# RWKV mixer of a hybrid decoder step: plain fp32 projections with r projected per pair, and chunk inverses doubled without VectorE transposes

## The chip, the cores and the metric

The program runs on one core of a Trainium2 chip. The metric is the device time of one launch in microseconds. TensorE (PE in the rows) multiplies, VectorE (DVE), ScalarE (ACT) and GpSimd (POOL) work on tiles of 128 partitions, SyncE (SP) issues most transfers. Every engine takes its own instructions in order; semaphores hold one until another engine is done.

## The reference, cut to what matters

One step of a two-layer trunk for 304 tokens: 16 meta and 256 prompt tokens of one sequence, and 8 samples of 4 tokens. The change is in the odd layer's mixer (RWKV-7); the even layer and the two PEER retrieval stages stay as they are.

```python
def rwkv7_mixer(x, s0, shift, ...):
    x_prev = jnp.concatenate([shift[:, None, :].astype(x.dtype), x[:, :-1]], axis=1)
    xx = x_prev - x
    xr, xw, xk, xv, xa, xg = (x + xx * mu[i] for i in range(6))
    r = xr @ w_r
    w = -jax.nn.softplus(-(w0 + jnp.tanh(xw @ w1) @ w2).astype(F32)) - 0.5
    k = xk @ w_k
    v = xv @ w_v
    a = jax.nn.sigmoid(a0 + (xa @ a1) @ a2)
    g = jax.nn.sigmoid(xg @ g1) @ g2
    ...
    y, s_new = wkv7_scan(rh, decay, kh, vh, -kk, kk * ah, s0)
    ...
    out = (y * g).astype(x.dtype) @ w_o
```

The scan is S = S diag(w) + (S a) b^T + v k^T, y = S r, for 16 heads of 64 channels. The kernel computes it in chunks of 64 tokens; in a chunk the (S a) terms are the solution of a triangular system, whose inverse the kernel builds.

## The kernel before, in words

Activations lie with 128 of 1024 channels on the partitions and the 304 tokens along the row; a weight block is 8 tiles of 128x128, 512 KB (`raw`). A product of full precision is made in one of two ways. Split: `wtile` (L243) and `split` (L169) make a rounded fp32r part and a residual of weights (`wh`, `wl`) and of activations (`mixh`, `mixl`), with ACT for the rounding and VectorE or GpSimd for the residual, and `mm3` (L174) makes three products. Plain: one fp32 product, which the trace shows as two passes.

`mixer1` (L1201) follows the layer normalization of the retrieval stage before it. Its prologue computes the six token-shift mixes (`blend`, L1348): k and v stay plain (`xk`, `xv`), the others are split. All eight r projections, the low-rank projections of w and a (one block) and that of g are made here in split form, then k, v and the preparation of pair 0.

The main part goes over eight pairs of heads with six generators per pair: `kv` (L1381, plain projections of k and v), `prep` (L1285, decays, normalized keys, `AR`, `BK`, `uv`), `attend` (L1470, products inside chunks), `inverse` (L1516), `chain` (L1591, the serial pass over five chunks) and `tail` (normalization and gate). Each step of each generator has a due number, pair + n0 + n1 * step (`self.mp`, L199), and the steps are issued in the order of these; the tile framework then places instructions in each engine's order. 144 small bf16 products into `ps_pj` (`warm`, L278) keep TensorE at work between them.

`inverse` works on three groups of the five chunks (2, 2 and 1 blocks of 128x128, two heads in each). It doubles the size of the inverted diagonal blocks in steps, on a matrix and its transpose (`ZV`), with a masked transposed block `t` (`tx`) as weights. The transposed block comes from a VectorE transpose of 32x32 squares out of PSUM (L1559), masked by a second VectorE instruction (L1560); the last steps use smaller transposes (L1564, L1572, L1574). At the end one correction step (L1584, L1588) refines the result. PSUM has eight banks: three of them (`iv`) serve the inverse, the attention products and part of the preparation in turn, two `ch`, and one each `mm`, `pu` and `pj`.

Of the kernel before, what the change touches and what calls it, by code (L numbers as in the profile page):

```python
# [8 lines left out]
F32 = mybir.dt.float32  # L9
# [11 lines left out]
P = 128  # L21
# [18 lines left out]
def _consts():  # L40
# [39 lines left out]
    for j in range(2):  # L80
# [11 lines left out]
        [ma[0].reshape(P, P), ma[1].reshape(P, P), lv[:, 0].T, lv[:, 1:5].reshape(P, 4 * P)], axis=1).astype(np.float32)  # L92
# [89 lines left out]
class Prog:  # L182
    def __init__(self, tc, a, es):
# [15 lines left out]
        self.mp = dict(q0=-3.6, q1=.12, p0=-3.0, p1=.14, a0=-2.2, a1=.14, i0=-1.45, i1=.2, c0=0, c1=.24, t0=1.5, t1=.15,  # L199
# [55 lines left out]
    def fetch(self, srcs):  # L255

        nc, tl = self.nc, lambda tag, dt: self.t(self.strm, [P, KB, P], dt, tag, 2)
        raws = [tl("raw", F32) for _ in srcs]
        for r, src in zip(raws, srcs):
            nc.sync.dma_start(r, src)  # L260

        def pre():
            self.turn.update(raw=-1, wh=1, wl=1)
            for j, r in enumerate(raws):
                h, l = tl("wh", F32R), tl("wl", F32R)
                split(nc, r, h, l, nc.gpsimd if j == 0 else None)
                self.ready.append((h, l))
        return pre
# [467 lines left out]
    def peer(self, xh, xl, l):  # L736
# [8 lines left out]
        with ExitStack() as es:  # L745
# [439 lines left out]
            pre = None if last else self.fetch([a["w_r"][j] for j in range(2)])  # L1185
# [15 lines left out]
    def mixer1(self, x, norm):  # L1201
        nc, a = self.nc, self.a
        with ExitStack() as es:
# [11 lines left out]
            masks = tl([P, 7, P], "masks", 1, BF16)  # L1215
            amask, lm0t, lmask = [masks[:, j, :] for j in range(2)], masks[:, 2, :], [masks[:, 2 + j, :] for j in range(5)]
# [18 lines left out]
            xkv = tl([P, KB, T], "xk"), tl([P, KB, T], "xv")  # L1235
# [49 lines left out]
            def prep(p):  # L1285
                AR, BK, uv = ARs[p % 6], BKs[p % 6], uvs[p % 6]
# [59 lines left out]
            mix, slot = {}, {0: 0, 1: 1, 4: 2, 5: 1}  # L1346

            def blend(i, k):  # L1348

                whole = 1 < i < 4  # L1350
                m = xkv[i - 2][:, k, :] if whole else ta([P, T], "sq", 3)
                nc.vector.scalar_tensor_tensor(m, xx[:, k, :], vec(7 + i, k), x[:, k, :], op0=ALU.mult, op1=ALU.add)  # L1352
                if whole:
                    return
                if k == 0:
                    mix[i] = tuple(ta([P, KB, T], f"{n}{slot[i]}", 1, F32R) for n in ("mixh", "mixl"))
                mh, ml = mix[i]
                split(nc, m, mh[:, k, :], ml[:, k, :], None if k % 4 == 1 else nc.gpsimd)

            srcs = [a["w_r"][p] for p in range(KB)] + [a["w_l1"][1]]  # L1360
            srcs.insert(5, a["w_l1"][0])
            tiles = []

            def weights():

                while len(tiles) < 3 and srcs:
                    tiles.append(self.wtile(srcs.pop(0), nc.gpsimd if len(srcs) % 3 == 0 else None))
                return tiles.pop(0)

            turn = [0]  # L1370

            def proj(w, i, c0=0, c1=P):
                turn[0] += 1
                ps = self.psum(("mm", "iv", "iv", "iv")[turn[0] % 4])
                wh, wl = w
                mh, ml = mix[i]
                mm3(nc, ps[:c1 - c0, :T], lambda k: wh[:, k, c0:c1], lambda k: wl[:, k, c0:c1],
                    lambda k: mh[:, k, :], lambda k: ml[:, k, :])
                return ps

            def kv(p):  # L1381

                for j, n in enumerate(("w_k", "w_v")):
                    w = self.stream("raw", F32)
                    nc.sync.dma_start(w, a[n][p])
# [5 lines left out]
                    nc.scalar.activation(Vts[p % 2][:, :T] if j else Kt[:, p, :], ps, AF.Copy)  # L1391
                    yield

            steps = [(i, k) for i in (1, 4, 2, 3, 5) for k in range(KB)]

            def ahead(n):
                for _ in range(n):
                    if steps:
                        blend(*steps.pop(0))


            ws, pr = [self.wtile(srcs.pop(0)) for _ in range(2)], [self.psum("iv") for _ in range(2)]
# [10 lines left out]
            def r(p, n):  # L1413
                ps = pr[p] if p < 2 else proj(weights(), 0)
                nc.scalar.activation(R[:, p, :], ps[:, :T], AF.Copy)
                ahead(n)

            r(0, 1)
            r(1, 1)
            for p in (2, 3, 4):  # L1420
                r(p, 5)
            w = weights()
            for i, c in ((1, 0), (4, 64)):
                ps = proj(w, i, c, c + 64)
                nc.scalar.activation(hwa[c:c + 64], ps[:64, :T], AF.Copy if c else AF.Tanh)
                ahead(4)
            gens = {}
            gens["q", 0], gens["p", 0] = kv(0), prep(0)
            for _ in range(5):
                next(gens["q", 0], None)  # L1430
                ahead(3)
            for p in (5, 6, 7):
                next(gens["p", 0], None)
                r(p, 4)
            ps = proj(weights(), 5)
            nc.scalar.activation(hg, ps[:, :T], AF.Sigmoid)
            for _ in gens["p", 0]:
                pass
            nc.vector.tensor_copy(psh.unsqueeze(2), x[:, :, TP - 1:TP])
# [11 lines left out]
            TX = 5  # L1451
            GROUPS = ((0, 2), (2, 2), (4, 1))

            for j in (2, 3, 4, 5, 1):
# [7 lines left out]
            X5s = [[tb([P, 2, P], f"x5{i}{j}") for j in range(2)] for i in range(2)]  # L1462
            for x5, X in X5s:
                nc.gpsimd.tensor_copy(x5, self.ident[:, None, :].to_broadcast([P, 2, P]))
                nc.gpsimd.memset(X, 0.0)
# [4 lines left out]
            def attend(p):  # L1470

                AR, BK, NT = ARs[p % 6], BKs[p % 6], NTs[p % 3]
# [41 lines left out]
                st[p] = AR, uvs[p % 6], AT, BT, NT, Ts, SA, SR  # L1514

            def inverse(p):  # L1516


                NT = NTs[p % 3]
                Zo = BKs[p % 6].rearrange("p c a t -> p c (a t)")  # L1520
                st[p] += (Zo,)
                wh, wl = self.t(self.strm, [P, KB, P], F32R, "wh", 2), self.t(self.strm, [P, KB, P], F32R, "wl", 2)
                flat = lambda ap: ap.rearrange("p c t -> p (c t)")
                gs = []
                for c0, n in GROUPS:
# [7 lines left out]
                    gs.append([c0, n, NR, ZV, t])  # L1533
                yield
                for j in range(6):
                    for g in gs:
                        c0, n, NR, ZV, t = g
# [3 lines left out]
                        bc = lambda ap: ap[:, None, :].to_broadcast([P, n, P])  # L1541
                        pz = self.psum("iv")
                        if j in (0, last):
                            pz = pz[:, :n * P].rearrange("p (c t) -> p c t", c=n)
                            for i in range(n):
                                mm(nc, pz[:, i, :], t[:, i, :], (NR if j == 0 else ZV[:, 0])[:, i, :], i == 0)
                            pv = pz
                            nc.scalar.activation(ZV[:, 1 if j == 0 else 0], pz, AF.Copy)
                        else:
                            pz = pz[:, :2 * n * P].rearrange("p (z c t) -> p z c t", z=2, c=n)  # L1550
                            for i in range(n):
                                mm(nc, pz[:, :, i, :], t[:, i, :], ZV[:, :, i, :], i == 0)
                            pv = pz[:, 1]
                            nc.scalar.activation(ZV, pz, AF.Copy)
                        if j < last:
                            t = g[4] = tb([P, 2, P], "tx", TX, F32R)[:, :n]
                            if j < 4:
                                x0 = tb([P, 2, P], "x0", TX)[:, :n]
                                nc.vector.transpose(flat(x0), flat(pv))  # L1559
# [236 lines left out]
```

## Time and profile before

| what | value |
|---|---|
| runs before | 2589.85 us median of 3 (2588.52 to 2590.93) |
| profiled execution | 2597.26 us, span of the core 2595.2 us |
| TensorE busy | 2437.2 us (94%) |
| VectorE busy | 1860.5 us (72%) |
| ACT, GpSimd busy | 1163.0 us (45%), 611.9 us (24%) |
| mean granted TensorE clock | 0.957 |

The page is one profiled execution. A matmul's end is modelled, so a busy TensorE may still have room; the granted clock is the share of full speed that the throttle allowed. The rows that the prediction uses follow in a section of their own.

### The profile page before, as it was taken

Reading aid. Unit: us, or ns where it says so; the run is one execution under the profiler, and the core shown is the slowest. Engines: PE = TensorE matmul, PEld = TensorE weight load, DVE = VectorE, ACT = ScalarE, POOL = GpSimd, SP = SyncE. Lnnn points to the kernel's source line nnn. Section 1 sums busy time; section 2 is a strip of 40 time slices with the busy share of each in tenths; the row PEclk is TensorE's granted clock in tenths of the full one; section 3 lists DMA queues with packets and bytes.
Section 4 is the critical chain, followed back from the end, with each engine's and each line's share of the span. In section 5 each row is a group of like instructions: output and inputs, shape, how many; then the busy total and the mean of one; then the engine's idle time right before and its main releaser. Section 6 shows DMA issues by size and latency. Waiting matters only on the chain.

```text
span 2595.2 us, 47120 instructions
## 1 busy us (share of the span) xinstructions
PE 2437.2 (94%) x18393; PEld 2232.2 (86%) x18402; DVE 1860.5 (72%) x4210; ACT 1163.0 (45%) x2092; POOL 611.9 (24%) x648
## 2 busy tenths in 40 slices
PE   7998999899999999977999988899989999999997
PEld 6887879799999999966666656797989999999996
DVE  5445898777767878767687785579777666677775
ACT  7424334444444444434554443432444444444453
POOL 3335200001111522036433422630010011051100
PEclk9868999999999999988998999899999999999998
DMA  5313246798889988732211002324679777798762
GB/s 165 107 52 135 90 151 229 263 318 280 276 276 302 360 280 283 237 106 80 72 36 38 32 20 92 119 78 134 235 259 296 252 250 247 259 328 267 247 220 84
DMA packets 197895, 490.09 MB, mean 189 GB/s; under 512 B 21397, under 2 KB 91429, under 8 KB 192937
## 3 DMA queue, kind: packets, MB, share of 16 engines
q1 hardware_dynamic: 173480, 401.10, 46.2%
q0 software_dynamic: 23040, 83.90, 9.6%
q8 instruction: 144, 2.36, 0.4%
q10 hardware_dynamic: 1152, 2.10, 0.2%
q14 instruction: 79, 0.64, 0.1%
HBM read 447.41 MB, written 39.63 MB: 188 GB/s over the span
## 4 chain that ended last, share of the span: by engine, by line
PE 75%; DVE 14%; ACT 3%; issue 3%; POOL 2%; DMA 2%; SPq 0%; POOLq 0%; ACTq 0%; DVEq 0%
PE ps_mm L162 34%; PE ps_u L162 24%; PE ps_s L162 8%; PE ps_iv L162 3%; PE ps_pj L162 3%; DMA gb<-G 2%; PE ps_ch L162 1%; PE ps_po L162 1%; ACT wh L170 1%; DMA raw<-in_ut 1%; DVE wl L171 1%; DVE sq L1352 1%; DVE ab L910 1%; DVE tx L1560 1%; POOL mixl L171 0%
## 5 line engine op out<-in xcount | busy, mean ns | idle before, releaser
L170 ACT ACTIVATE wh<-raw 128x1024 fp32r<-128x1024 f32 x539 | 570.9, 1060 | 777.4 <-PE ps_mm L162 332.2
L171 DVE TENSOR_TENSOR wl<-raw,wh 128x1024 fp32r<-128x1024 f32 x487 | 609.3, 1251 | 356.0 <-ACT wh L170 340.8
L162 PE MATMUL ps_u<-xh,wh 128*128 128x256 f32 x1664 | 472.6, 284 | 3.6 <-ACT act L990 2.6
L162 PE MATMUL ps_u<-xh,wl 128*128 128x256 f32 x1664 | 470.1, 282 | 4.2 <-DVE wl L171 4.2
L162 PE MATMUL ps_u<-xl,wh 128*128 128x256 f32 x1664 | 468.3, 281 | 0.0
L162 PE MATMUL ps_mm<-sc,wh 128*128 128x256 f32 x1984 | 351.6, 280 | 13.0 <-ACT sc L170 13.0
L162 PE MATMUL ps_mm<-qs,wh 128*128 128x256 f32 x1984 | 361.0, 283 | 0.0
L162 PEld LDWEIGHTS ps_u<-xh,wh 128*128 128x128 f32 x1664 | 315.5, 190 | 5.2 <-ACT act L990 3.0
L162 PEld LDWEIGHTS ps_u<-xh,wl 128*128 128x128 f32 x1664 | 314.9, 189 | 5.2 <-DVE wl L171 5.0
L162 PEld LDWEIGHTS ps_u<-xl,wh 128*128 128x128 f32 x1664 | 315.0, 189 | 1.0 <-issue 0.8
L162 PEld LDWEIGHTS ps_mm<-sc,wh 128*128 128x128 f32 x1984 | 304.1, 190 | 13.4 <-ACT sc L170 13.4
L162 PEld LDWEIGHTS ps_mm<-qs,wh 128*128 128x128 f32 x1984 | 306.4, 190 | 0.1
L1076 POOL DMA_INDIRECT ab<-in_u,er x80 | 79.6, 995 | 865.2 <-DVE ab L1083 481.3
L162 PE MATMUL ps_mm<-qs,wl 128*128 128x256 f32 x992 | 279.8, 283 | 0.0
L162 PE MATMUL ps_mm<-sc,wl 128*128 128x256 f32 x992 | 276.9, 279 | 0.0
L1076 POOL DMA_INDIRECT ab<-in_v,er x80 | 129.8, 1622 | 409.1 <-DVE gb L1097 325.5
L162 PEld LDWEIGHTS ps_mm<-sc,wl 128*128 128x128 f32 x992 | 188.6, 190 | 0.1
L162 PEld LDWEIGHTS ps_mm<-qs,wl 128*128 128x128 f32 x992 | 188.2, 190 | 0.2
L171 POOL TENSOR_TENSOR wl<-raw,wh 128x1024 fp32r<-128x1024 f32 x52 | 126.0, 2428 | 76.5 <-ACT wh L170 68.8
L162 PE MATMUL ps_mm<-xh,wh 128*128 128x304 f32 x416 | 135.3, 329 | 8.0 <-ACT xh L342 4.2
L990 ACT ACTIVATE act<-ps_u 128x256 f32<-128x256 f32 x256 | 94.2, 369 | 106.6 <-PE ps_u L162 106.5
L162 PE MATMUL ps_s<-ab 128*128 128x128 f16 x1024 | 133.4, 296 | 1.7 <-ACT gb L959 1.3
(556 smaller groups left out, 4666.5 us busy)
## 6 DMA issues: line engine op xcount, KB each, us to landing
raw<-in_ut SPq DMA_DIRECT2D x256, 512.0 KB
raw<-in_v SPq DMA_DIRECT2D x256, 512.0 KB
G<-gb SPq DMA_DIRECT2D x32, 1024.0 KB
gb<-G SPq DMA_DIRECT2D x32, 1024.0 KB
raw<-in_wq SPq DMA_DIRECT2D x32, 512.0 KB
raw<-in_w_in SPq DMA_DIRECT2D x20, 512.0 KB
raw<-in_w_out SPq DMA_DIRECT2D x8, 512.0 KB
raw<-in_w_r SPq DMA_DIRECT2D x8, 512.0 KB
```

Of the source, the lines that this page charges most:

```text
L162: nc.tensor.matmul(out, lhsT, rhs, start=start, stop=stop, skip_group_check=True)
L170: nc.scalar.activation(h, src, AF.Copy)
L171: return (eng or nc.vector).tensor_tensor(l, src, f(h), op=ALU.subtract)
L910: nc.vector.tensor_tensor(eqj, eqj, ib[:n, :, None, :].to_broadcast([n, 16, 16, nh]), op=ALU.mult)
L990: nc.scalar.activation(acts[e], pu, AF.Gelu_apprx_tanh)
L1076: nc.gpsimd.indirect_dma_start(out=w[:, j, :], out_offset=None, in_=a[f"{tab}{l}"], in_offset=bass.IndirectOffsetOnAxis(ap=gst[g][0][:, c ...
L1352: nc.vector.scalar_tensor_tensor(m, xx[:, k, :], vec(7 + i, k), x[:, k, :], op0=ALU.mult, op1=ALU.add)
L1560: nc.vector.tensor_tensor(t, x0, bc(lmask[j + 1]), op=ALU.mult)
```

## The change

Two edits, made together. First, the mixer's projections are all plain fp32. The blocks fetched ahead during the retrieval stage are now that of w and a and that of k for pair 0, unsplit (`fetch_whole`); w, a and k of pair 0 follow the normalization tile by tile, then come r and v of pair 0 and g. The mix for r is kept (`xr`), and r of the pairs 1 to 7 is projected between k and v of its pair (`krv`). Second, `inverse` gets its transposed blocks from TensorE: each step makes the next matrix (`pz`) and a product `pu` that already is the transpose needed for the next step, in a second PSUM tile; VectorE masks it on the way out of PSUM. The first uses an identity in fp32r (`eye`), and the final transpose is TensorE's own. Sets of pair buffers go from six to five, `tx` buffers from five to four, and `i1` from 0.2 to 0.16, since `inverse` has nine steps for seven.

```diff
+    def fetch_whole(self, srcs):
+        raws = [self.t(self.strm, [P, KB, P], F32, "raw", 2) for _ in srcs]
+        for r, src in zip(raws, srcs):
+            self.nc.sync.dma_start(r, src)
+        def pre():
+            self.turn.update(raw=1, wh=-1, wl=-1)
+            self.ready.extend(raws)
+        return pre
...
-            pre = None if last else self.fetch([a["w_r"][j] for j in range(2)])
+            pre = None if last else self.fetch_whole([a["w_l1"][0], a["w_k"][0]])
...
-                split(nc, m, mh[:, k, :], ml[:, k, :], None if k % 4 == 1 else nc.gpsimd)
...
+            def krv(p):
+                for n, i, dst in (("w_k", 2, Kt[:, p, :]), ("w_r", 0, R[:, p, :]), ("w_v", 3, Vts[p % 2][:, :T])):
+                    w = block(a[n][p])
+                    ps = self.psum("pj")[:, :T]
                     for k in range(KB):
-                        mm(nc, ps, w[:, k, :], xkv[j][:, k, :], k == 0, k == KB - 1)
+                        mm(nc, ps, w[:, k, :], xof[i][:, k, :], k == 0, k == KB - 1)
                         if k == 3:
                             yield
+                    nc.scalar.activation(dst, ps, AF.Copy)
...
             for k in range(KB):
                 norm(k)
                 before(k)
-                blend(0, k)
-                for (wh, wl), ps in zip(ws, pr):
-                    for j, (w, y) in enumerate(((wh, mix[0][0]), (wh, mix[0][1]), (wl, mix[0][0]))):
-                        mm(nc, ps[:, :T], w[:, k, :], y[:, k, :], k + j == 0, k + j == KB + 1)
+                for j, i in enumerate((1, 4)):
+                    mm(nc, p1[j][:64, :T], w1[:, k, 64 * j:64 * j + 64], blend(i, k), k == 0, k == KB - 1)
+                mm(nc, pk, wk[:, k, :], blend(2, k), k == 0, k == KB - 1)
...
-                    nc.vector.tensor_tensor(ZV[:, 0], f(NR), bc(lm0t), op=ALU.mult)
-                    nc.vector.transpose(flat(x0), flat(f(ZV[:, 0])))
-                    nc.scalar.activation(t, x0, AF.Copy)
+                    pu = v(self.psum("iv"))
+                    for i in range(n):
+                        mm(nc, pu[:, i, :], ZV[:, 1, i, :], eye, i == 0)
+                    t = tb([P, 2, P], "tx", TX, F32R)[:, :n]
+                    nc.vector.tensor_tensor(t, pu, bc(lmask[0]), op=ALU.mult)
...
-                                x0 = tb([P, 2, P], "x0", TX)[:, :n]
-                                nc.vector.transpose(flat(x0), flat(pv))
-                                nc.vector.tensor_tensor(t, x0, bc(lmask[j + 1]), op=ALU.mult)
...
+                            pu = v(self.psum("iv"))
                             for i in range(n):
+                                mm(nc, pu[:, i, :], ZV[:, 1, i, :], t[:, i, :], i == 0)
...
+                            nc.vector.tensor_tensor(g[3], pu, bc(lmask[j + 1]), op=ALU.mult)
+                            nc.scalar.activation(ZV, z, AF.Copy)
...
-                            for q in (0, 64):
-                                nc.vector.transpose(X[q + 32:q + 64, :, q:q + 32], z[q:q + 32, :, q + 32:q + 64])
-                                for o in (q, q + 32):
-                                    nc.vector.transpose(X[o:o + 32, :, o:o + 32], z[o:o + 32, :, o:o + 32])
...
+                    for i in range(n):
+                        nc.tensor.transpose(px[:, i, :], f(ZV[:, 0, i, :]), self.ident)
...
-            steps_of = dict(q=(kv, 4), p=(prep, 5), a=(attend, 5), i=(inverse, 7), c=(chain, 6), t=(tail, 4))
+            steps_of = dict(q=(krv, 6), p=(prep, 5), a=(attend, 5), i=(inverse, 9), c=(chain, 6), t=(tail, 4))
```

TensorE at the first two tiles after the normalization, before: three products per weight block and tile, two r blocks, `mixh` and `mixl` being the parts of one mix.

```order
L162 MATMUL ps_iv_12557<-mixh_1872_12567,wh_12480 128x304
L162 MATMUL ps_iv_12557<-mixl_1873_12568,wh_12480 128x304
L162 MATMUL ps_iv_12557<-mixh_1872_12567,wl_12481 128x304
L162 MATMUL ps_iv_12558<-mixh_1872_12567,wh_12484 128x304
L162 MATMUL ps_iv_12558<-mixl_1873_12568,wh_12484 128x304
L162 MATMUL ps_iv_12558<-mixh_1872_12567,wl_12485 128x304
```

The same place now: per tile one product each for w and a (64 columns of weights, mixes `sq`) and one for k of pair 0 (`xk`).

```order
L162 MATMUL ps_iv_12550<-sq_12559,raw_12314 64x304
L162 MATMUL ps_iv_12551<-sq_12562,raw_12314 64x304
L162 MATMUL ps_pj_12552<-xk_12512,raw_12315 128x304
L162 MATMUL ps_iv_12550<-sq_12573,raw_12314 64x304
L162 MATMUL ps_iv_12551<-sq_12576,raw_12314 64x304
L162 MATMUL ps_pj_12552<-xk_12512,raw_12315 128x304
```

The mixes are no longer split, and r's products have left this place. The second place is a doubling step of pair 0's inverse on VectorE; before, with `x` the transposed and `tx` the masked block:

```order
L1560 TENSOR_TENSOR tx_13473<-x_2031_13474,masks_12505 128x256
L1559 STREAM_TRANSPOSE x_2034_13482<-ps_iv_13477 128x256
L1559 STREAM_TRANSPOSE x_2037_13489<-ps_iv_13485 128x128
L1560 TENSOR_TENSOR tx_13481<-x_2034_13482,masks_12505 128x256
L1560 TENSOR_TENSOR tx_13488<-x_2037_13489,masks_12505 128x128
```

The same step on VectorE now, and the one after the attention's evictions (`AT`):

```order
L1538 TENSOR_TENSOR tx_13047<-ps_iv_13040,masks_12497 128x256
L1538 TENSOR_TENSOR tx_13058<-ps_iv_13051,masks_12497 128x256
L1538 TENSOR_TENSOR tx_13066<-ps_iv_13062,masks_12497 128x128
L1465 TENSOR_TENSOR AT_13074<-ps_iv_13075,masks_12497 128x256
L1465 TENSOR_TENSOR AT_13074<-ps_iv_13076,masks_12497 128x256
```

One instruction per group and step stands where two stood. The third place is TensorE in such a step, `wl` and `wh` holding the matrices; before:

```order
L162 MATMUL ps_iv_13543<-wl_13390,tx_13473 128x2x128 x2
L162 MATMUL ps_iv_13551<-wl_13390,tx_13481 128x2x128 x2
L162 MATMUL ps_pj_13639<-xk_12520,raw_13637 128x304
L162 MATMUL ps_mm_13530<-k_all,rnb_12537 128x128 x2
L162 MATMUL ps_mm_13530<-k_all,rnb_12537 128x48
L162 MATMUL ps_iv_13559<-wh_13389,tx_13488 128x256
```

And now, where the rows with `tx` ahead of `wl` are the added products:

```order
L162 MATMUL ps_iv_13162<-tx_13093,wl_13014 128x128 x2
L162 MATMUL ps_iv_13161<-wl_13014,tx_13093 128x2x128
L162 MATMUL ps_mm_13147<-hwa_12504,wa_1853_12525 128x304
L162 LDWEIGHTS k_all
L162 MATMUL ps_pj_13159<-k_all 128x512
L162 MATMUL ps_iv_13161<-wl_13014,tx_13093 128x2x128
L162 MATMUL ps_iv_13170<-wl_13014,tx_13102 128x2x128 x2
L162 MATMUL ps_iv_13179<-wh_13013,tx_13109 128x256
L162 MATMUL ps_mm_13196<-hwa_12504,wa_1853_12525 128x304
L162 MATMUL ps_iv_13171<-tx_13102,wl_13014 128x128 x2
```

Each group's step writes two `ps_iv` tiles instead of one.

## Rows read from the trace of the kernel before

**Rows 1.** The page's chain that ended last, whole span, share by engine

```profile
PE 75%; DVE 14%; ACT 3%; issue 3%; POOL 2%; DMA 2%; SPq 0%; POOLq 0%; ACTq 0%; DVEq 0%
```

**Rows 2.** Table of stages; columns are the view's own first line

```profile
core 0: us, PE busy (x) PEld busy (x) DVE busy (x) ACT busy (x) POOL busy (x), PEclk, DMA share, GB/s
1151.00:1239.50 88.50, 67.68 (x339) 54.91 (x338) 63.70 (x99) 37.15 (x76) 53.24 (x90) 0.87 0.26 82
1239.50:1602.50 363.00, 336.51 (x2583) 230.32 (x2591) 271.39 (x803) 172.64 (x496) 130.04 (x191) 0.96 0.12 39
1340.70:1436.60 95.90, 90.09 (x636) 61.18 (x633) 70.17 (x210) 42.14 (x126) 32.14 (x51) 0.86 0.12 37
1477.40:1557.50 80.10, 71.05 (x618) 45.46 (x622) 66.32 (x196) 38.98 (x111) 28.26 (x36) 0.98 0.06 20
```

**Rows 3.** The chain from 1151.0 to 1239.5 us, share by line

```profile
by line: DVE sq L1352 15.6%; POOL mixl L171 14.5%; PE ps_iv L162 9.7%; PE ps_mm L162 7.4%; PE ps_pj L162 4.6%; issue 4.2%; POOL wl L171 3.1%; DVE xv L1352 3.0%; ACT mixh L170 2.6%; DVE xl L333 2.6%; DVE xk L1352 2.3%; DVE AR L1312 2.2%; POO
```

**Rows 4.** Costliest groups from 1151.0 to 1239.5 us; busy, mean ns | idle before

```profile
L171 POOL TENSOR_TENSOR mixl<-sq,mixh 128x304 fp32r<-128x304 f32 x24 | 27.3, 1150 | 14.7 <-ACT mixh L170 14.7
...
L1352 DVE SCALAR_TENSOR_TENSOR sq<-xx,vm,xh 128x304 f32<-128x304 f32 x32 | 23.1, 756 | 3.9 <-POOL mixl L171 2.2 <-POOL xx L1264 1.6
...
L1262 DVE TENSOR_TENSOR xx<-xh 128x303 f32<-128x303 f32 x8 | 4.5, 575 | 0.0
...
L334 DVE SCALAR_TENSOR_TENSOR xl<-ps_u,lnv,xl 128x304 f32<-128x304 f32 x8 | 4.1, 526 | 0.0
L333 DVE SCALAR_TENSOR_TENSOR xl<-xl,lnv,ps_u 128x304 f32<-128x304 f32 x8 | 4.0, 522 | 2.5 <-PE ps_u L162 2.5
```

**Rows 5.** The chain from 1239.5 to 1602.5 us, share by line

```profile
by line: PE ps_pj L162 18.6%; PE ps_iv L162 17.3%; PE ps_ch L162 8.3%; PE ps_mm L162 8.0%; issue 7.2%; DVE tx L1560 3.7%; DVE x L1574 3.3%; PE ps_pu L162 3.1%; DVE x L1559 2.2%; DVE BK L1320 1.8%; DVE x L1572 1.6%; POOL rns L1276 1.5%; ACT 
```

**Rows 6.** VectorE in order of time, 1139 to 1145 us; start, length

```profile
1139.94 2.61 DVE L364 TENSOR_TENSOR xl<-xl,ab 128x304 f32<-128x304 f32 x1
1142.48 0.46 DVE L371 TENSOR_TENSOR ab<-ab 128x304 f32<-128x304 f32 x1
...
1143.63 1.21 DVE L171 TENSOR_TENSOR wl<-raw,wh 128x1024 fp32r<-128x1024 f32 x1
```

**Rows 7.** GpSimd in order of time, 1125 to 1178 us

```profile
1139.64 2.58 POOL L171 TENSOR_TENSOR wl<-raw,wh 128x1024 fp32r<-128x1024 f32 x1
```

**Rows 8.** VectorE's groups from 1239.5 to 1602.5 us

```profile
L1560 DVE TENSOR_TENSOR tx<-x,masks 128x256 fp32r<-128x256 f32 (+1 forms) x88 | 42.9, 507 | 0.4
L1559 DVE STREAM_TRANSPOSE x<-ps_iv 128x256 f32<-128x256 f32 (+1 forms) x88 | 33.4, 398 | 9.1 <-ACT wl L1554 4.9 <-ACT wl L1548 3.8
...
L1484 DVE TENSOR_TENSOR AT<-ps_iv,masks 128x256 f32<-128x256 f32 (+1 forms) x48 | 16.8, 375 | 20.2 <-PE ps_iv L162 19.5
L1574 DVE STREAM_TRANSPOSE x<-wl 32x64 f32<-32x64 f32 x64 | 15.1, 235 | 0.9
...
L1564 DVE STREAM_TRANSPOSE x<-ps_iv 32x64 f32<-32x64 f32 x32 | 7.8, 244 | 6.3 <-ACT wl L1554 5.6
L1572 DVE STREAM_TRANSPOSE x<-wl 32x64 f32<-32x64 f32 x32 | 7.5, 236 | 1.2 <-ACT wl L1548 0.5
L1531 DVE STREAM_TRANSPOSE x<-wl 128x256 f32<-128x256 f32 x16 | 6.8, 435 | 0.2
L1530 DVE TENSOR_TENSOR wl<-wh,masks 128x256 fp32r<-128x256 f32 x16 | 6.7, 424 | 4.2 <-POOL wh L1529 4.1
...
L1312 DVE SCALAR_TENSOR_TENSOR AR<-kk,Dp 128x320 f32<-128x320 f32 x7 | 5.9, 847 | 1.1 <-ACT Dp L1300 1.0
```

**Rows 9.** TensorE in order of time, two places

```profile
1235.31 4.26 PE L162 MATMUL ps_pj<-xk,raw 128*128 128x304 f32 x16
1239.50 1.16 PE L162 MATMUL ps_iv<-AR,BK 64*128 64x128 f32 x12
...
1520.00 0.77 PE L1498 MATMUL ps_iv<-k_all,BK 128*128 128x128 f32 x5
1520.70 0.34 PE L162 MATMUL ps_ch<-uv,AT 128*64 128x64 f32 x4
```

More of the change, by code (lines that the diff above doesn't have):

```diff
@@ L1214, in mixer1 @@
             o2 = ck[:, o + 73:]
[L1215 to L1216 removed]
+            masks = tl([P, 8, P], "masks", 1, BF16)
+            amask, lmask = [masks[:, j, :] for j in range(2)], [masks[:, 2 + j, :] for j in range(6)]
             vm = self.vm1
@@ L1344, in prep @@
                     nc.gpsimd.memset(uv[r, 0, h, :], 0.0)
-            mix, slot = {}, {0: 0, 1: 1, 4: 2, 5: 1}
+            xof = {0: xr, 2: xkv[0], 3: xkv[1]}
             def blend(i, k):
-                whole = 1 < i < 4
-                m = xkv[i - 2][:, k, :] if whole else ta([P, T], "sq", 3)
+                m = xof[i][:, k, :] if i in xof else ta([P, T], "sq", 4)
                 nc.vector.scalar_tensor_tensor(m, xx[:, k, :], vec(7 + i, k), x[:, k, :], op0=ALU.mult, op1=ALU.add)
[L1353 to L1357, printed above, removed]
-                split(nc, m, mh[:, k, :], ml[:, k, :], None if k % 4 == 1 else nc.gpsimd)
@@ L1360, in mixer1 @@
[L1360 to L1385, printed above, removed]
+                return m
+            def block(src):
+                if self.ready:
+                    return self.ready.pop(0)
+                w = self.stream("raw", F32)
+                nc.sync.dma_start(w, src)
+                return w
+            def krv(p):
+                for n, i, dst in (("w_k", 2, Kt[:, p, :]), ("w_r", 0, R[:, p, :]), ("w_v", 3, Vts[p % 2][:, :T])):
+                    w = block(a[n][p])
@@ L1396, in ahead @@
[L1396 to L1402, printed above, removed]
+            w1, wk = block(None), block(None)
+            p1, pk = [self.psum("iv") for _ in range(2)], self.psum("pj")[:, :T]
             for k in range(KB):
@@ L1427, in mixer1 @@
-            gens = {}
[L1428 to L1436, printed above, removed]
+            nc.scalar.activation(hwa[:64], p1[0][:64, :T], AF.Tanh)
+            nc.scalar.activation(hwa[64:], p1[1][:64, :T], AF.Copy)
@@ new lines, in mixer1 @@
+            nc.scalar.activation(Kt[:, 0, :], pk, AF.Copy)
+            gens = {}
+            gens["q", 0], gens["p", 0] = iter(()), prep(0)
+            first_r, first_v = block(a["w_r"][0]), block(a["w_v"][0])
+            wg = block(a["w_l1"][1])
+            for i, w, dst in ((0, first_r, R[:, 0, :]), (3, first_v, Vts[0][:, :T])):
+                ps = self.psum("pj")[:, :T]
+                for k in range(KB):
+                    blend(i, k)
+                    mm(nc, ps, w[:, k, :], xof[i][:, k, :], k == 0, k == KB - 1)
+                    if k == 4 and i == 0:
+                        next(gens["p", 0])
+                nc.scalar.activation(dst, ps, AF.Copy)
+                if i == 0:
+                    next(gens["p", 0])
@@ L1437, in mixer1 @@
+            pg = self.psum("iv")[:, :T]
+            for k in range(KB):
+                mm(nc, pg, wg[:, k, :], blend(5, k), k == 0, k == KB - 1)
+                if k == 1:
+                    next(gens["p", 0])
             for _ in gens["p", 0]:
                 pass
+            nc.scalar.activation(hg, pg, AF.Sigmoid)
             nc.vector.tensor_copy(psh.unsqueeze(2), x[:, :, TP - 1:TP])
@@ L1461, in mixer1 @@
             nc.gpsimd.memset(nts[:, :15 * P + 4 * 64], 0.0)
[L1462 to L1465, printed above, removed]
+            eye = tb([P, P], "eye", 1, F32R)
+            nc.scalar.activation(eye, self.ident, AF.Copy)
             grs = tb([P, 3, 2], "rs")
@@ L1719, in mixer1, with weights, proj @@
             es.callback(self.extra, None, 0, 0)
-            srcs.extend(a["w_o"][p] for p in range(NB, KB))
-            mix[6] = y
+            srcs, tiles = [a["w_o"][p] for p in range(NB, KB)], []
+            def weights():
+                while len(tiles) < 3 and srcs:
+                    tiles.append(self.wtile(srcs.pop(0), nc.gpsimd if len(srcs) % 3 == 0 else None))
+                return tiles.pop(0)
+            def proj(m):
+                ps = self.psum("iv" if m % 4 else "mm")
+                wh, wl = weights()
+                mm3(nc, ps[:, :T], lambda k: wh[:, k, :], lambda k: wl[:, k, :],
+                    lambda k: y[0][:, k, :], lambda k: y[1][:, k, :])
+                return ps
             x = tc_([P, KB, T], "x")
@@ L1725, in mixer1 @@
             for m in range(KB):
-                pz = pr[m] if m < NB else proj(weights(), 6)
+                pz = pr[m] if m < NB else proj(m)
                 if m == 7:
```

115 lines of the change are left out of this document (47 added, 68 removed).

## The prediction

> **What bounds the kernel now.** I read the page's chain of waits first, then a table of stages, then for each stage its own chain, the costliest groups and a few stretches in order of time. Over the whole span the chain runs 75% through TensorE [rows 1], but that is the retrieval stages, which the change leaves alone. The RWKV mixer lies between 1151.0 and 1602.5 us and has two parts.
>
> The first, 1151.0 to 1239.5 (the prologue: token-shift mixes, the r, w, a and g projections, the first preparation), is 88.5 us long. TensorE, VectorE and GpSimd are busy 67.7, 63.7 and 53.2 us of it, at a mean granted clock of 0.87 [rows 2]: nobody is full. Its own chain says why: a mix on VectorE (sq, 15.6%) is split on ACT and GpSimd (mixl, 14.5%) before TensorE may go on [rows 3]. A residual on GpSimd takes 1150 ns; meanwhile mixes on VectorE average 756 ns, where the normalization's instructions of the same kind and size, with one operand in PSUM, take 522 to 526 [rows 4].
>
> The second, 1239.5 to 1602.5 (the main part: eight pairs of heads in a software pipeline), is 363.0 us long. TensorE is busy 336.5 us (93%), VectorE 271.4 (75%), ACT 172.6 [rows 2]. The busy row of TensorE holds modelled ends, so it is no proof that TensorE is full. The chain is mixed: the five largest TensorE pieces make 55.3% of it (18.6, 17.3, 8.3, 8.0 and 3.1), four VectorE pieces of the inverse 10.8% (3.7, 3.3, 2.2 and 1.6), and 7.2% is issue [rows 5]. From 1477.4 to 1557.5 VectorE is busy 66.3 of 80.1 us [rows 2]. So main is paced by two in-order engines that wait for one another, and the change takes work from one and gives work to the other.
>
> **The normalization before the mixer.** The two splits of w_r weights in its last step go. One is a GpSimd residual of 2.58 us at 1139.64, beside which a VectorE subtraction takes 2.61 us; the next VectorE instruction with 304 columns takes 0.46. The other is 1.21 us on VectorE at 1143.63, just ahead of the statistics [rows 6, 7]. Bounds: nothing (TensorE's statistics come late anyway) to 2.15 + 1.21 = 3.4 us. I take 2.
>
> **The prologue.** Removed: all splits of weights and mixes, the 24 GpSimd residuals of 1150 ns among them, and seven of the eight r projections. Left on VectorE are, by the order of the changed program, 16 normalization instructions (16 x 0.525 = 8.4 us), 8 differences (8 x 0.575 = 4.6), 48 mixes and twelve instructions of the first preparation. Without GpSimd's residuals beside them I price a mix as the normalization's same form, 48 x 0.525 = 25.2; for the twelve I take at most the 847 ns of their widest, 10.2 [rows 4, 8]. The sum is 48 us. TensorE has 24 + 24 plain fp32 products there, each two passes of 0.26 us (16 passes from 1235.31 to 1239.50 are 4.19 us [rows 9]): 48 x 0.52 = 25 us, and 50 even at the 1.2 GHz level, which is under or about VectorE's sum. So VectorE becomes the bound and the part is 48 us instead of 88.5: minus 40. Below: the mixes and everything else overlap better and it is 43. Above: the preparation's serial steps stand behind the last mix, and it is 62. The loads of these weights are fewer than before and stand in SP's queue ahead of the store of x, as the order shows; no wait of theirs is priced.
>
> **r in the main part.** Seven blocks of 16 passes move there: 7 x 4.19 = 29.3 us of TensorE, each with an ACT eviction that was in the prologue before. Each block's 512 KB load stands in SP's queue between those of k and v, and the three now share two buffers. Main's DMA share is 0.12 [rows 2], and no wait of a k or v product for a load is among the listed pieces of the chain, so I count the load at nothing; if that cover goes, TensorE stands in order behind it.
>
> **The inverse.** Per pair VectorE loses the transposes, the masking of their results and the first mask. The seven largest groups are 42.9 + 33.4 + 15.1 + 7.8 + 7.5 + 6.8 + 6.7 = 120 us over all pairs. It gains 16 masked evictions out of PSUM per pair, 128 in all. Nearest is the attention's masked eviction, same operands and shapes, 375 ns as a mean over its two widths; the new ones are wide more often, so 128 x 0.385 = 49 us [rows 8]. VectorE's net is minus 71 us, but what counts is what lies on the chain [rows 5]: 10.8% of 363 = 39 us goes, and the new evictions come back at the place of L1560 (3.7% = 13.4 us, times 49 / 42.9 = 15). That is minus 24.
>
> TensorE gains 38 products of 128 columns per pair: 5 first products with the identity, 5 more for the other half of step 0, 23 that make the next transposed block, 5 final transposes; 304 in all. Five full-size transposes from 1520.00 to 1520.70 took 0.14 us each, and twelve half-height ones from 1239.50 took 1.16, or 0.10 each [rows 9]. So 30 to 43 us; the new ones are full size, I take 43. The removed ACT copies (40) and the new ones (24, and 8 for r) about cancel on an engine that is busy 173 of 363 us.
>
> What do 29 + 43 = 72 us more on TensorE cost? Its pieces are 55.3% of the chain, so an average microsecond costs at least 0.55; where it is already the bound, 1. I take 0.65, nearer to the lower end, since shorter VectorE stalls leave idle places to fill: 47 us. Main is 363 + 47 - 24 = 386.
>
> Fewer buffers (five sets per pair for six, four tx for five), the earlier spacing of the inverse's steps and the longer mask constant I count at nothing: the preparation that reuses a set stands after the tail of its last user in the table of due numbers, and the other edits touch no listed piece of the chain. If that cover is gone, GpSimd and VectorE wait in a preparation, which is inside the range.
>
> **Sum.** -2 - 40 + 23 = -19 us. The profiled execution took 2597.26 us (span 2595.2), so 2578 by it. The runs shown have a median of 2589.85, some 7 us lower, and the forecast is 2589.85 - 19 = 2571 us. Its own range, 2552 to 2584, is the prologue's and the normalization's bounds with 0.55 to 0.8 for TensorE.
>
> **Rivals.**
> Rival A, slower: TensorE sets the pace of main and VectorE's relief is worth nothing. The place is the "iv" group of three PSUM banks. A pair takes 52 tiles of it instead of 33 (the inverse alone 41 instead of 22), and within a step one group's two products now hold two of the three banks, so TensorE, which goes in order, stands until an eviction is done. For it: TensorE is busy 93% already. Against it: each step of the doubling was two VectorE instructions long and is now one. Main is 363 + 72 = 435, the total -42 + 72 = +30: 2620 us. It decides as soon as main grows by more than 42 us.
>
> Rival B, no gain: the clock. From 1340.7 to 1436.6 the granted clock was 0.86, partly at 1.2 instead of 2.4 GHz, although TensorE was busy 90.1 of 95.9 us [rows 2]. If all of main ran so instead of at 0.96, its listed TensorE pieces (201 us) would grow by 0.96/0.86, or 23 us: 2571 + 23 = 2594. Against it: TensorE gets more work in these stretches, not less. The Trainium skill (TensorE: Matmul & The Clock Gate, section "A second HAM failure mode: psum-queue depth-cycling") describes a kernel whose clock kept falling because it went round PSUM banks with small idle gaps; the stretch at 0.86 looks like that, and by this rule more tiles through the same three banks speak for rival B.
>
> Rival C, more: the pipeline was held by VectorE. TensorE's additions cost 0.55 of their lower price (59 x 0.55 = 33), and the whole 39 us on the chain goes, since the new evictions hide: main 357, total -42 - 6 = -48, 2542 us. For it: 66.3 of 80.1 us in the late stretch.
>
> Rival D: the prologue only falls to 62 us, because the mixes, now without splits, still alternate with the serial preparation: -2 - 26 + 23 = -5, 2585 us.
>
> **How the numbers follow.** Forecast 0.42, A 0.21, B 0.10, C 0.17, D 0.10. A measurement of this kernel can tell about 0.2%, 5 us, from no change. Faster: 0.40 of the forecast, all of C, 0.04 of D: 0.61. Slower: A and 0.08 of B: 0.29. Same: the rest, 0.10. The range goes from 2536, a little past C, to 2616, short of A's full price: about 0.1 is left out at either side.
>
> **What would show it.** Right: from the first LN instruction to the first attention product some 48 us instead of 88.5 with VectorE nearly full and GpSimd nearly idle; main some 386 us with VectorE's share near 50% and TensorE's products of "ps_pj" and "ps_iv" on the chain. A shows as TensorE waits of "ps_iv" for ACT and VectorE evictions and a main of 420 or more; B as a clock under 0.9 through main; C as a main of 360 or less; D as gaps on VectorE in the prologue behind GpSimd's powers and ACT's activations. The prediction is wrong in its core if the prologue doesn't shrink by 26 us, or if main grows by more than 42.

## The result, and the profile after

The changed kernel takes 2616.86 us (median of 4 runs, 2614.83 to 2620.67) against 2590.39 us before (4 runs beside them, 2588.52 to 2592.81): a ratio of 1.0102, 95% interval 1.0086 to 1.0117. The forecast was 2571 us with a range up to 2616. It is slower by 26 us, which is nearly what rival A priced (2620).

The profiled execution has a span of 2616.4 us, 21.2 more than before. I divide it at the same events as before: first the table of stages (prologue, main, and main's late stretch), then main of the kernel before, which here ends at the start of the last pair's output (0.4 us earlier than in [rows 2]).

```profile
core 0: us, PE busy (x) PEld busy (x) DVE busy (x) ACT busy (x) POOL busy (x), PEclk, DMA share, GB/s
1142.60:1190.10 47.50, 38.54 (x137) 21.71 (x137) 39.32 (x86) 14.56 (x31) 19.43 (x55) 0.91 0.23 76
1190.10:1626.20 436.10, 410.77 (x2992) 295.22 (x3006) 205.13 (x571) 178.13 (x487) 128.87 (x193) 0.96 0.13 40
1476.00:1568.90 92.90, 87.48 (x649) 63.03 (x654) 45.27 (x135) 37.05 (x103) 26.46 (x36) 0.85 0.05 17
```

```profile
1239.50:1602.10 362.60, 336.11 (x2573) 229.99 (x2583) 271.39 (x803) 172.64 (x496) 129.79 (x190) 0.96 0.12 38
```

Against [rows 2]: the prologue fell from 88.5 to 47.5 us (-41.0; forecast -40). Main grew from 362.6 us to 436.1 (+73.5; forecast +23). What lies before the prologue ended 8.5 us earlier, what lies behind main is 2.9 us shorter: -8.5 - 41.0 + 73.5 - 2.9 = +21.1. In main TensorE's busy share went from 93 to 94%, VectorE's from 75 to 47%, at the same mean clock of 0.96; only the low stretch moved (the late stretch ran at 0.98 before and at 0.85 now). TensorE's idle time in main is 436.1 - 410.8 = 25.3 us, and it was 26.5 before.

The chain of main by line, for [rows 5], and the costliest new VectorE groups with what VectorE waited for:

```profile
by line: PE ps_pj L162 27.5%; PE ps_iv L162 24.8%; PE ps_ch L162 9.4%; PE ps_mm L162 7.9%; issue 5.5%; PE ps_pu L162 4.2%; DVE kk L1325 2.2%; DVE BK L1331 1.7%; POOL rns L1287 1.6%; ACT wl L1539 1.3%; POOL rs L1287 1.2%; DVE BK L1332 1.1%; 
```

```profile
L1538 DVE TENSOR_TENSOR tx<-ps_iv,masks 128x256 fp32r<-128x256 f32 (+1 forms) x104 | 40.6, 392 | 56.8 <-PE ps_iv L162 56.1
...
L1516 DVE TENSOR_TENSOR tx<-ps_iv,masks 128x256 fp32r<-128x256 f32 (+1 forms) x24 | 8.3, 375 | 17.9 <-PE ps_iv L162 17.9
```

```profile
DVE tx L1538 <- PE ps_iv L162: 56.1, 60, 3.4
...
PEld ps_iv L162 <- ACT wl L1539: 9.1, 23, 0.9
...
PEld ps_iv L162 <- ACT x L1552: 4.0, 4, 1.2
...
PE ps_iv L162 <- ACT wl L1539: 3.6, 11, 0.8
```

The largest such waits of the kernel before were for VectorE:

```profile
PEld ps_iv L162 <- DVE x L1559: 4.5, 9, 1.0
...
PE ps_iv L162 <- DVE tx L1560: 3.7, 3, 1.7
```

The five TensorE pieces went from 55.3 to 73.8% of the chain, and no VectorE piece of the inverse is among those that the line lists (all over 1%). VectorE's busy time fell by 66 us (forecast 71). The new evictions cost 40.6 + 8.3 = 48.9 us (forecast 49), and VectorE now stands 56.1 + 17.9 us in front of them, waiting for TensorE. The other way round, the waits of the inverse's products for an engine are short, and they changed sides: 9.1, 4.0 and 3.6 us for ACT's evictions now, 4.5 and 3.7 us for VectorE before, when none for ACT is listed.

The prologue's groups answer to [rows 4]:

```profile
L1362 DVE SCALAR_TENSOR_TENSOR sq<-xx,vm,xh 128x304 f32<-128x304 f32 x24 | 12.2, 546 | 0.7 <-POOL xx L1275 0.6
L1362 DVE SCALAR_TENSOR_TENSOR xk<-xx,vm,xh 128x304 f32<-128x304 f32 x8 | 4.2, 522 | 0.0
...
L1362 DVE SCALAR_TENSOR_TENSOR xv<-xx,vm,xh 128x304 f32<-128x304 f32 x8 | 3.8, 524 | 0.0
L1362 DVE SCALAR_TENSOR_TENSOR xr<-xx,vm,xh 128x304 f32<-128x304 f32 x8 | 3.7, 524 | 0.0
```

Without the residuals on GpSimd a mix takes 522 to 546 ns instead of 756. For the normalization, VectorE's last residual of the stage before and the first instruction behind the statistics:

```profile
1118.97 1.23 DVE L171 TENSOR_TENSOR wl<-raw,wh 128x1024 fp32r<-128x1024 f32 x1 [1.62 <-ACT wh L170]
...
1142.59 0.97 DVE L344 SCALAR_TENSOR_TENSOR xl<-xl,lnv,ps_u 128x304 f32<-128x304 f32 x2 [2.55 <-PE ps_u L162]
```

The same two of the kernel before:

```profile
1125.52 1.23 DVE L171 TENSOR_TENSOR wl<-raw,wh 128x1024 fp32r<-128x1024 f32 x1 [1.62 <-ACT wh L170]
...
1151.07 0.97 DVE L333 SCALAR_TENSOR_TENSOR xl<-xl,lnv,ps_u 128x304 f32<-128x304 f32 x2 [2.55 <-PE ps_u L162]
```

25.55 us between them before, 23.62 after: the forecast's -2. The other 6.5 us by which the prologue starts earlier lie ahead of these rows, and little of them is the change's: in six runs below with the old projections the same residual starts between 1120.0 and 1122.7 us, in e1_proj, with the new ones, at 1121.2. The execution of the kernel before that was profiled was long there (its 2597.26 us are 7 above the median).

### The profile page after: what moved, and what is told of

Read it like the earlier page. It is cut to its first block, busy times and chain, and to the rows that moved or that the text cites. A ratio compares the mean times of both kernels' runs of the same rounds, so it can differ in the third digit from the quotient of the medians.

```text
span 2616.4 us, 47266 instructions
## 1 busy us (share of the span) xinstructions
PE 2472.7 (95%) x18603; PEld 2254.6 (86%) x18618; DVE 1771.6 (68%) x3964; ACT 1143.4 (44%) x2035; POOL 567.5 (22%) x616
## 4 chain that ended last, share of the span: by engine, by line
PE 77%; DVE 12%; DMA 4%; ACT 3%; issue 3%; POOL 2%; SPq 0%; POOLq 0%; ACTq 0%; DVEq 0%
PE ps_mm L162 33%; PE ps_u L162 23%; PE ps_s L162 7%; PE ps_pj L162 5%; PE ps_iv L162 4%; DMA gb<-G 2%; PE ps_ch L162 2%; DVE wl L171 1%; PE ps_po L162 1%; DMA raw<-in_ut 1%; PE ps_pu L162 1%; ACT wh L170 1%; DVE ab L921 1%; DVE ab L923 0%; DVE ab L918 0%
## 5 line engine op out<-in xcount | busy, mean ns | idle before, releaser
L170 ACT ACTIVATE wh<-raw 128x1024 fp32r<-128x1024 f32 x529 | 560.6, 1060 | 776.7 <-PE ps_mm L162 404.2
L171 DVE TENSOR_TENSOR wl<-raw,wh 128x1024 fp32r<-128x1024 f32 x481 | 602.4, 1253 | 353.6 <-ACT wh L170 339.1
L1087 POOL DMA_INDIRECT ab<-in_v,er x80 | 122.7, 1534 | 416.3 <-DVE gb L1108 332.6
L171 POOL TENSOR_TENSOR wl<-raw,wh 128x1024 fp32r<-128x1024 f32 x48 | 115.0, 2400 | 89.9 <-ACT wh L170 72.9
```

Source lines behind the costliest of these rows:

```text
L170: nc.scalar.activation(h, src, AF.Copy)
L171: return (eng or nc.vector).tensor_tensor(l, src, f(h), op=ALU.subtract)
L1087: nc.gpsimd.indirect_dma_start(out=w[:, j, :], out_offset=None, in_=a[f"{tab}{l}"], in_offset=bass.IndirectOffsetOnAxis(ap=gst[g][0][:, c ...
```

## The experiments

Theory 1: in main, TensorE's own work sets the pace, so each microsecond added to it lies on the path and VectorE's relief is worth little. Theory 2: the inverse's products wait for the three iv banks (rival A's place). Theory 3: TensorE's granted clock, which the 144 warm products hold up, decides. Below, "main" runs from the first attention product to the last pair's output; its row stands under each run, with the columns of the table above. Ratios are to the kernel before, run beside each.

**One part at a time.** e1_proj is the changed kernel with the old inverse, its masks and its spacing; e2_inv is the kernel before with the new inverse:

```
e1_proj, against the changed kernel:
-steps_of = dict(q=(krv, 6), ..., i=(inverse, 9), ...
+steps_of = dict(q=(krv, 6), ..., i=(inverse, 7), ...   # inverse, masks, X5s as before
e2_inv, against the kernel before:
-steps_of = dict(q=(kv, 4), ..., i=(inverse, 7), ...
+steps_of = dict(q=(kv, 4), ..., i=(inverse, 9), ...    # inverse, masks, eye as changed
```

> The projections' part of the change alone, with the old inverse. All theories: prologue 48 us instead of 88.5, normalization 2 us shorter. Theory 1 (in the main part every microsecond added to TensorE lies on the path): main 363 + 29 = 392 us, total 2590 - 42 + 29 = 2577 us. Theory 2 (the inverse's products wait for the three iv banks; r uses none of them): r costs its 0.65 as forecast, main 382, total 2567 us.

> The inverse's part alone, with the old projections. Prologue unchanged at 88 us. Theory 1: main 363 + 43 = 406 us, total 2633 us. Theory 2: the banks make it dearer than its products, main 417, total 2644 us. By the factor of the prediction (43 x 0.65 - 24 = +4) it would be 2594 us.

e1_proj: 2570.2 us, ratio 0.9936 (0.9911 to 0.9960). e2_inv: 2659.3 us, ratio 1.0270 (1.0240 to 1.0299); its profiled execution, 2672.7 us, was the longest of six. Main of e1_proj, then of e2_inv:

```profile
1192.40:1580.60 388.20, 362.38 (x2695) 246.51 (x2702) 271.84 (x803) 175.81 (x503) 131.73 (x193) 0.97 0.14 45
```

```profile
1235.50:1674.30 438.80, 417.08 (x2874) 302.97 (x2894) 200.93 (x571) 175.20 (x480) 124.60 (x191) 0.86 0.10 32
```

Either run has the buffers of the kernel that its projections come from, and the inverse's spacing goes with the inverse; neither was tried by itself. The projections' part is a gain of 19 us and beats both kernels: main grows by 25.6 us for r's 29.3. The inverse's part alone is a loss of 70, more than either theory said, and its main ran at a clock of 0.86. So -19 and +70 don't add up to the +26 of both; the clock has to be taken out first.

**The clock between two executions of one program.** e10_inv_again is e2_inv and e11_after_again the changed kernel, unchanged, one execution each, on a chip on which the kernel before took 2592.0 us.

> e2_inv once more, for the clock of a second execution. Theory 3: main at 0.90 or less again, total 2650 to 2675 us. If it is 0.95 or more, the total is 2620 to 2635 us and the clock of e2_inv was one of chance.

> The changed kernel once more, for the clock of a second execution. Theory 1: main 436 within 6 us at a clock of 0.95 to 0.97, total 2611 to 2622 us.

2652.6 and 2635.6 us; main of e10_inv_again, then of e11_after_again:

```profile
1234.20:1655.90 421.70, 402.62 (x2895) 290.06 (x2894) 200.37 (x571) 174.59 (x480) 124.48 (x191) 0.91 0.10 33
```

```profile
1189.40:1644.10 454.70, 432.41 (x3007) 306.81 (x3006) 205.26 (x571) 178.36 (x487) 129.15 (x193) 0.91 0.12 39
```

The expectation for the changed kernel missed: it was 44 us slower than the kernel before here, not 26, and its main was 18.6 us longer at 0.91 than at 0.96. The inverse's was 17.1 us shorter at 0.91 than at 0.86. So part of main's clock is the execution's, not the program's. Call length x (1 - clock) the clock lost in main: 17.4 and 40.9 us in the changed kernel, 61.4 and 38.0 us in e2_inv. If the clock is the whole difference, one microsecond of it costs 18.6/23.5 = 0.79 or 17.1/23.4 = 0.73 us of time. With 0.76 I bring each main to full clock (the clock's two decimals leave about 2 us open): before 351.6, e1_proj 379.3, e2_inv 392.1 and 392.9, the changed kernel 422.8 and 423.6. At full clock r costs 27.7 us, the inverse 40.5 alone and 43.5 beside r, and both 71.2. The 0.76 comes from these two pairs, so that each pair agrees after it shows nothing, and that it holds for the other kernels is assumed. Lost clock counted over the whole span, a straight line through all runs of one kernel (their span against it) has a slope of 0.54 for the kernel before (52 runs), 0.73 for e7_proj_iv4 (10) and 0.99 for e3_nowarm (4). With anything from 0.54 to 1 in place of 0.76, differences between mains at 0.95 to 0.97 move by 1.5 us or less either way; the inverse alone lies between 29 and 51.

**The products' price and VectorE's relief, each by itself.** e5_twice issues the old inverse's products twice; e6_notrans leaves its VectorE transposes out, and with them correct inverses:

```
e5_twice, at each of the four loops of products:
-for i in range(n):
+for _ in range(2):
+    for i in range(n):
...
e6_notrans, at steps 0 to 3 (the later transposes go the same way):
-nc.vector.transpose(flat(x0), flat(pv))
-nc.vector.tensor_tensor(t, x0, bc(lmask[j + 1]), op=ALU.mult)
+nc.vector.tensor_tensor(t, pv, bc(lmask[j + 1]), op=ALU.mult)
```

> The kernel before with each of the inverse's 304 products issued twice (the second overwrites the first with the same values); VectorE's work is as before. About 304 x 0.12 = 36 us more on TensorE. Theory 1 (at the same clock each added microsecond lies on the path): main 363 + 36 = 399, total 2626 us, and more if the granted clock of main falls under 0.96. The prediction's factor 0.65: main 386, total 2613 us.

> The kernel before without the DVE transposes of the inverse (its masks then read PSUM directly; the inverses it computes are left out by that), so VectorE loses some 75 us and TensorE's work is as before. Theory 1: TensorE paces main, the relief is worth nothing: main 357 to 366, total 2583 to 2592 us. The prediction's credit of 24 us: main 339, total 2566 us.

e5_twice: 2649.2 us, ratio 1.0242 (1.0207 to 1.0278). e6_notrans: 2579.3 us, ratio 0.9968 (0.9948 to 0.9988). Main of e5_twice, then of e6_notrans:

```profile
1234.00:1656.50 422.50, 390.74 (x2927) 284.56 (x2934) 274.23 (x803) 174.74 (x496) 129.93 (x191) 0.93 0.10 33
```

```profile
1234.80:1585.10 350.30, 335.39 (x2582) 231.69 (x2590) 198.28 (x555) 172.03 (x496) 127.87 (x191) 0.95 0.12 40
```

In e5_twice TensorE's busy time grew by 54.6 us and main by 59.9, at 0.93; at full clock that is 400.0 - 351.6 = 48.4 us (45 to 52 with 1 and 0.54 for 0.76), 0.16 each: nothing of it was hidden, and it is dearer than the 36 expected. These are as many products as the change adds, but not the same: 144 of the 304 have 256 columns and 40 take two passes, where the change's all have 128 columns, as a row of e5_twice and one of the changed kernel show:

```profile
L162 PE MATMUL ps_iv<-wl,tx 128*128 128x256 f32 x256 | 56.9, 335 | 3.3 <-DVE tx L1562 3.1
```

```profile
L162 PE MATMUL ps_iv<-tx,wl 128*128 128x128 f32 x160 | 39.8, 316 | 6.7 <-ACT wl L1539 3.4 <-ACT x L1552 3.2
```

So 48.4 is a price near the change's, not the change's. In e6_notrans VectorE lost 73 us of work. Main changed by 337.0 - 351.6 = -14.6 us and the kernel by -9: more than theory 1's nothing, well short of the prediction's 24. TensorE was as busy as before, and its idle time in main fell from 26.5 to 14.9 us.

**The same relief beside r.** e13_proj_notrans is the same edit in e1_proj.

> The projections' part alone, without the DVE transposes of the inverse (the inverses it computes are left out by that), so VectorE loses some 75 us beside r. Theory 1 with a relief that shrinks as TensorE fills up: main 377 to 388 us, total 2560 to 2570. The relief of the run without r (9 us of time, 14 at the same clock) in full: main 374, total 2557. The prediction's credit of 24 us: main 364, total 2546 us.

```profile
1193.50:1574.20 380.70, 361.84 (x2700) 251.54 (x2702) 204.74 (x555) 175.82 (x503) 129.37 (x194) 0.97 0.14 46
```

2564.8 us, ratio 0.9909 (0.9877 to 0.9941). At e1_proj's clock main is 7.5 us shorter (7.3 at full clock): the relief of 14.6 is halved once r's blocks are there. TensorE's idle time fell from 25.8 to 18.9 us. VectorE is left as busy as in the changed kernel (204.7 and 205.1 us). If its relief there is the same 7.3, the change's own products cost 43.5 + 7.3 = 51 us.

**Banks.** e4_iv4 gives the changed kernel a fourth iv bank, e7_proj_iv4 gives e1_proj one:

```
-self.psum_banks(iv=3, ch=2, mm=1, pu=1, pj=1)
+self.psum_banks(iv=4, ch=2, mm=1, pj=1)
...
-pr, pT, py = (pc[:, 64 * j:64 * j + 64] for j in range(3))
+pr, pT, py, pu = (pc[:, 64 * j:64 * j + 64] for j in range(4))
...
```

> The changed kernel with four iv banks for three (the chain's u product moves into the chain's own bank, which frees one). Theory 1: TensorE's work is the same, main within 6 us of 436, total 2610 to 2617. Theory 2: the waits for banks shrink, main falls to 400 or less, total 2580 or less.

> The projections' part alone, with four iv banks. Theory 1: TensorE's work is the same as in e1_proj, total 2565 to 2571 us. Theory 2: waits for the banks take part of its time, main shrinks by 10 to 16 us, total 2554 to 2560 us.

e4_iv4: 2611.6 us, ratio 1.0090 (1.0057 to 1.0123). e7_proj_iv4: 2572.4 us, ratio 0.9933 (0.9912 to 0.9954). Main of e4_iv4, then of e7_proj_iv4:

```profile
1191.60:1619.20 427.60, 399.95 (x2986) 288.71 (x3005) 203.33 (x571) 174.45 (x487) 127.25 (x193) 0.94 0.13 41
```

```profile
1190.30:1579.50 389.20, 361.50 (x2689) 248.90 (x2699) 271.42 (x803) 175.55 (x503) 129.01 (x193) 0.93 0.14 45
```

Neither time differs from that without the bank. At full clock (408.1 and 368.5) the bank is worth 14.7 and 10.8 us, about alike with 52 and with 33 tiles a pair, but the granted clock was lower with it and took that back. So theory 2 explains 14.7 - 10.8 = 4 us of what the new inverse costs, or none: the clock's decimals leave as much open.

**Warm products, fewer and more.** `fe` and `fl` set their spacing: 0 issues none (e3_nowarm, changed kernel); .2 and .05 issue 103 (e8_proj_w103 in e1_proj, and e14_proj_iv4_w103 in e7_proj_iv4); .1 and .0233 issue 217 (e9_inv_w217 in e2_inv, e12_before_w217 in the kernel before).

> The changed kernel without the 144 warm products of 512 columns (their results are used by nothing). Theory 1: TensorE is the bound, so 144 x 0.37 us come off: main 436 - 53 = 383, total 2564 us, if the granted clock stays at 0.96; if it falls to 0.86, the listed TensorE pieces (323 us) grow by 38 and the total is 2602. Theory 2: the warm products fill waits for banks, so nothing changes: 2612 to 2617.

> The projections' part alone with 103 warm products for 144. Theory 1 with the clock held at 0.97 through main: 41 x 0.37 = 15 us off, total 2555 us. Theory 3 (TensorE's granted clock, which the warm products hold up, decides): the clock of main falls under 0.92 and gives the 15 us back, total 2568 to 2585 us.

> The inverse's part alone with 217 warm products for 144: 73 x 0.37 = 27 us more on TensorE, in the run whose main was granted a clock of 0.86. Theory 1 alone (each added microsecond costs one, the clock as in e2_inv): main 439 + 27 = 466, total 2686 us. Theory 3 (what made e2_inv dearer than its products is the clock, which added products hold up): the clock of main rises to 0.95 or more, main 415 to 430, total 2635 to 2655 us.

> The kernel before with 217 warm products for 144: 27 us more on TensorE that nothing waits for. Theory 1 at the same clock (0.96): main 363 + 27 = 390, total 2617 us. Theory 3: the clock of main rises to 1.00, which gives back 13 of the 27: total 2603 us. The prediction's factor 0.65: 2607 us; if idle places take them, 2590 us.

> The projections' part alone with four iv banks and 103 warm products. Theory 1 with the bank's share, at the clock of e1_proj: 12 us for the bank and 14 for the products off, main 362, total 2544 us. Theory 3: the granted clock of main falls under 0.93 and gives it back, total 2562 to 2578 us.

| run | us | ratio (95%) | main at full clock | against its parent |
|---|---|---|---|---|
| e3_nowarm | 2651.0 | 1.0246 (1.0211 to 1.0282) | 385.5 | -37.3 for 144 fewer |
| e8_proj_w103 | 2573.6 | 0.9941 (0.9921 to 0.9961) | 371.5 | -7.8 for 41 fewer |
| e9_inv_w217 | 2674.1 | 1.0309 (1.0277 to 1.0341) | 416.9 | +24.8 for 73 more |
| e12_before_w217 | 2630.6 | 1.0172 (1.0132 to 1.0211) | 381.2 | +29.6 for 73 more |
| e14_proj_iv4_w103 | 2573.6 | 0.9938 (0.9914 to 0.9961) | 364.7 | -14.6 with the bank |

Their mains, in this order:

```profile
1188.10:1659.60 471.50, 450.56 (x2862) 334.17 (x2862) 200.97 (x571) 179.47 (x487) 126.94 (x193) 0.76 0.12 37
```

```profile
1192.50:1578.70 386.20, 357.70 (x2652) 249.23 (x2661) 271.76 (x803) 176.13 (x503) 130.33 (x194) 0.95 0.14 46
```

```profile
1236.60:1680.50 443.90, 427.80 (x2968) 301.81 (x2967) 201.15 (x571) 175.40 (x480) 125.71 (x191) 0.92 0.10 32
```

```profile
1235.70:1635.10 399.40, 372.71 (x2664) 247.57 (x2663) 274.54 (x803) 175.34 (x496) 129.83 (x190) 0.94 0.11 35
```

```profile
1192.00:1583.50 391.50, 358.32 (x2652) 251.34 (x2661) 272.75 (x803) 176.82 (x503) 129.86 (x194) 0.91 0.14 45
```

Work that nothing waits for costs 0.34 to 0.41 us per warm product when added, where the expectation priced it at 0.37: theory 1, with a factor of one (27 to 32 us in e12_before_w217 with 1 and 0.54 for 0.76). Here no step of the inverse waits for the added products, as it may in e5_twice. Taken away, a product gives back less, 0.26 in e3_nowarm and 0.19 in e8_proj_w103; the first is far from the clocks that 0.76 was taken at (16 to 60 us with 0.54 and 1), so theory 1 is not shown for taking work away. Taking all away lets the clock fall to 0.76, and main is 35 us longer: theory 3 holds there. More of them did not clearly raise the clock: 0.92 against 0.86 and 0.91 in e9_inv_w217, 0.94 against 0.96 in e12_before_w217; theory 3's expectations for these two missed. Whether the 0.91 to 0.95 of e7, e8 and e14 comes of their edits or of the execution is not shown, but their other runs speak for the edits: over the whole span the clock was 0.954 to 0.963 in the 25 runs of these three and 0.964 to 0.966 in the six of e1_proj, though on other chips.

## Why the prediction was wrong, point by point

**Normalization and prologue: right in size, the prologue in part by luck.** -2 was -1.9, -40 was -41.0. But the 48 us were a sum of VectorE's work alone, and VectorE was busy 39.3 of the 47.5 us: the mixes had their price (23.9 us for 25.2), the preparation and the rest cost less than my upper bounds. In the last 7.9 us, from 1182.2, TensorE was busy all the time and VectorE for 2.0, a tail that the sum did not have. GpSimd was busy 19.4 us, not nearly idle. TensorE's 38.5 us lie between my 25 and 50. Rival D (62) is out.

**What TensorE's added work costs: the factor was wrong, and this is the step that failed.** It is "What do 72 us more on TensorE cost? ... I take 0.65". Its reason, that TensorE's pieces are only 55% of the chain and shorter VectorE stalls leave idle places, fell in e5_twice and e12_before_w217: work added to the kernel before, with VectorE's stalls as they were, came out whole. The other 45% of the chain were not time in which TensorE stood idle: it was busy 336.1 of the 362.6 us. The busy 93% that I set aside as modelled was the better guide. The sizes that went into the 72 were right or low: r was 29.3 us by count and costs 27.7 at full clock (with the fewer buffers); the inverse's 304 products I priced at 43 us, and they come to about 51, if the relief is as measured in e13_proj_notrans.

**VectorE's relief: wrong size.** "That is minus 24" took the VectorE pieces of the chain as time that comes back. Alone it was 14.6, beside r 7.3. The rows had the limit: with TensorE's work unchanged, main can win no more than TensorE's idle time as the trace shows it, which was 26.5 us before [rows 2], and a relief of 73 us of VectorE's work took 11.6 of that, or 6.9 beside r.

**The miss, summed.** Predicted for main: 19 + 28 - 24 = 23. Measured at full clock: 27.7 for r and 43.5 for the inverse, 71.2, and 73.5 as it ran. Of the 48 us between, the factor is 72 x 0.35 = 25, the relief 17 and the price of the products 8, with r's price 2 the other way. With the factor alone put right the forecast would have been 2596, so the relief and the price were needed for the miss too. The forecast's own range, 2552 to 2584, is not what its bounds add up to: they give 2557 (-3.4, -45.5, +15.6) to 2597 (0, -26.5, +33.6).

**The rivals.** A had the price (main 435, measured 436.1) and the point from which it decides, but not the place: TensorE's waits for ACT appeared, yet its idle time did not grow, and a fourth bank did not change the time, so it is the work that costs, not the banks. That its 72 us fit is in part luck: the products cost more than its 43 and the relief gave back something. B: the clock of main was 0.96 in both compared executions, so it is not the cause of this result; with the same 52 tiles a pair it was 0.96, 0.91, 0.86 and 0.91 in four executions with 144 warm products. The rule of the Trainium skill (TensorE: Matmul & The Clock Gate, section "A second HAM failure mode: psum-queue depth-cycling"), that going round PSUM banks with small idle gaps can keep the clock falling, is neither shown nor excluded by these. C is out: e6_notrans, which has VectorE's whole relief and none of the products, reached only 2579.

## What to carry to other kernels

In a stage like this one, where one engine was busy 93% and had 55% of the chain of waits, work added to it came out at a factor of one: price it so, and not by its share of the chain. What relieving a second engine can bring is limited by the idle time of the first, here 26.5 us, of which a relief of 73 us took 11.6, and less once the first was fuller. A change of two parts is best priced and run part by part: here one part wins 19 us and the other loses 70 alone, and only the first is worth keeping.

## What the runs showed of the hardware that was not expected

The mean granted clock of one stage of one program differed between executions (0.96 and 0.91; 0.86 and 0.91), and with it that stage by 17 to 19 us, as much as some of the effects in question; one profile of each kernel does not tell such differences apart from the clock's. Without the warm products main's clock fell to 0.76, although TensorE's busy share rose to 450.6 of 471.5 us.
